# Two transformer blocks on one core: both feed-forwards over all 1024 rows as seven block products, behind all attention

## The chip, the cores and the metric

One core of a Trainium2 chip (trn2). The metric is device time of one execution in microseconds: median 2538.9, three runs from 2533.7 to 2539.64. Engines: TensorE (PE, its weight loads PEld), VectorE (DVE), ScalarE (ACT), GpSimd (POOL), and SyncE (SP), whose queue issues the DMAs.

## The reference

Two different blocks run one after the other on x of 1024 rows x 1024 columns, float32. The first one has 16 more rows in front (`meta`), four heads of differential attention beside a state-space branch; the second has eight heads of causal attention with a forget gate beside a spatial gating branch. Each ends in the same way, and this is what the change touches:

```python
mix = concat(a, b) @ w_out                       # 1024 x 1024
h   = h + rmsnorm(mix, post_mix_g)
n   = rmsnorm(h, pre_ffn_g)
f   = silu(n @ w_gate) * (n @ w_up)              # 1024 x 2816
h   = h + rmsnorm(f @ w_down, post_ffn_g)        # 2816 x 1024
```

## The kernel before

**Matmuls.** Every large product is made of three: each operand is split into hi (rounded to the fp32r type by an ACT copy) and lo (the rest, a DVE subtraction), and hi x hi, hi x lo and lo x hi are summed in one PSUM bank (`mm3`, L106). `wpiece` (L97) brings a weight piece of 128x1024 by DMA into `wr` (2 buffers) and splits it into `wh` and `wl` (4 buffers each); `split` (L169) does the same for what comes out of a transpose.

**Staging.** Attention runs in two halves of 512 rows. In each block the first half (`attention(blk, 0, ...)`) runs beside the projections, and the second half is a generator (`second_half`, L901; `second_half2`, L1190): the last five units of the projections (`dense`), `attention(blk, 1, None)`, then `mix_out` (L769), which brings the attention output (`oD`, `o2D`) and the other branch back from DRAM, transposes them, multiplies by `w_out` and stores rows to `mixD`.

**Feed-forward.** `ffn` (L910) takes two halves of 512 rows. First it drains `mix_out` for rows 0 to 511 and normalises these rows (`norm_row`: `post_norm` L181, `norm_T` L148). Then, for each half, 22 tiles of 128 hidden columns in chunks of 6, 6, 6 and 4: `up` makes gate and up (2 x 8 x 3 matmuls of 128x512), `down` multiplies a chunk by `w_down` for 4 row tiles x 2 column halves and adds into `acc` in SBUF. During half 0 one `step(side)` of the generator above is traced after each tile, so that second-half attention, its mix and the feed-forward of the first half stand side by side. `post_norm` ends each row tile: square and sum on ACT, the power on POOL (L134), a scaling and the residual addition on DVE, a store. Rows 4 to 7 of the second block's input are normalised behind the first block's end (`pre_row`, L1007).

**Attention of a row tile.** `scores` (L607) makes the scores of one map or head in `s` (one PSUM buffer of 128x1024 in this phase), DVE adds the bias and takes the minimum (L626, in the second block after a mask addition L624), ACT takes the exponentials (L632). `transposed_product` (L650) transposes them on PE (L657), copies them to SBUF (L603 on ACT, L605 on DVE, in turn) and multiplies by the values (L118).

**Order.** No order is written by hand. A planner simulates the program at build time and writes each engine's list: what is traced earlier goes first, `ahead()` raises a stretch, and what is not ready in its simulation is passed over. On the chip each engine works its list off in order.

Of the kernel before, what the change touches and what calls it, by code (L numbers as in the profile page):

```python
# [22 lines left out]
KT = 8  # L23
# [7 lines left out]
FF_CHUNKS = [6, 6, 6, 4]  # L31
# [24 lines left out]
def tile_two_blocks(ctx: ExitStack, tc: tile.TileContext, a, out):  # L56
# [4 lines left out]
    wpool = ctx.enter_context(tc.tile_pool(name="wpool", bufs=4))  # L61
# [30 lines left out]
    cD = dram.tile([8, NX], F32, name="cD")  # L92

# [17 lines left out]
    class Bank:  # L111
        """Several sums in one PSUM bank: the first matmul clears it, the last one follows all others."""
# [35 lines left out]
    def norm_T(wk, pt, xt, g_bc, dst, col, np_=128):  # L148
        """Row tile xt [np_, 1024] -> normalised, times g, transposed into dst[hi, lo][:, :, col:col+np_]."""
# [31 lines left out]
    def post_norm(wk, mix, g_bc, res_src, dst, rt, cuts=1):  # L181
        """Row tile mix [128, 1024], normalised, times g, plus the residual; into dst and returned."""
# [3 lines left out]
        hx = wk.tile([128, 1024], F32, tag="hx", name="hx")  # L186
# [16 lines left out]
    # ---------------------------------------------------------------- first block: projections, S5  # L203
# [19 lines left out]
    psum_t = psum(ctx, "t", 2)  # L223
    psum_o = psum(ctx, "o", 1)
    psum_d = psum(ctx, "d", 2)
    psum_e = psum(ctx, "e", 1)
    psum_x = ExitStack()
    psum_s = [psum(psum_x, "s", 2)]

    def psum_phase(width):  # L230
        psum_x.close()
        psum_s[0] = psum(psum_x, "s", 1024 // width, width)

# [11 lines left out]
    rows_out = ctx.enter_context(tc.tile_pool(name="ev", bufs=4, reuse_waits="tile"))  # L245
    atp = ctx.enter_context(tc.tile_pool(name="atp", bufs=2, reuse_waits="tile"))
    lam = ctx.enter_context(tc.tile_pool(name="lam", bufs=1, reuse_waits="tile"))
# [23 lines left out]
    with ExitStack() as pre:  # L271
# [13 lines left out]
        # lambda  # L285
# [13 lines left out]
    # ---- S5 tables  # L299
# [114 lines left out]
    # D on the diagonal of the first tap, [h', g, h]  # L414
# [12 lines left out]
    def ssm_set(s):  # L427
# [15 lines left out]
        # chunk phases E[c], c = 16 a + b  # L443
# [8 lines left out]
        # input map: Gm[p, j, r', h'] = A^(7-r') Bb  # L452
# [8 lines left out]
        # output map: CA[p, j, n, h] = Re(C A^n), -Im(C A^n)  # L461
# [23 lines left out]
        # taps, then the block Toeplitz of a chunk  # L485
# [15 lines left out]
        # u of the set, transposed  # L501
# [19 lines left out]
        # chunk inputs to the states, both parts  # L521
# [53 lines left out]
    def dense1(half):  # L575
# [709 lines left out]
```

## Time and profile before

| | |
|---|---|
| median of 3 runs (lowest, highest) | 2538.9 us (2533.7, 2539.64) |
| span of the profiled execution | 2536.1 us |
| own time of the profiled execution beside its span | not given by the page; the runs' median is 2.8 us above the span |
| PE busy | 2468.3 us, 97% |
| DVE, ACT, POOL busy | 50%, 42%, 12% |
| DMA | 301.59 MB, 119 GB/s |
| mean granted TensorE clock | 0.989 |

A busy matmul counts from its start to a modelled end, and the next one starts before that end; the distance between starts, not the duration, is what one costs. Idle time of an engine that is not the bottleneck costs nothing.

### The profile page before, as it was taken

The numbers are of one execution on the slowest core, as the hardware profiler recorded it, in microseconds if no ns is written. First come the engines' busy times: TensorE is split into PE (matmuls) and PEld (weight loads), VectorE is DVE, ScalarE is ACT, GpSimd is POOL, SyncE is SP. The second block draws the span as 40 slices with busy tenths as digits, with TensorE's granted clock in tenths as the row PEclk, the third lists the DMA queues.
The fourth block names the chain that finished last, engine by engine and source line by source line (L and its number), as shares of the span: only waits on it lengthen the run. The fifth ranks groups of instructions, "written<-read, shape, count | busy, mean of one in ns | idle before, by whom it ended". The sixth has DMA issues, their size and how long they took to land. (4 is left out here: it accounts for less than half of the span.)

```text
span 2536.1 us, 30581 instructions
## 1 busy us (share of the span) xinstructions
PE 2468.3 (97%) x11808; PEld 2015.8 (79%) x11808; DVE 1256.3 (50%) x2035; ACT 1075.9 (42%) x1696; POOL 297.8 (12%) x308
## 2 busy tenths in 40 slices
PE   8998889999999999999999999999999999999998
PEld 6766667888888878888887888888888888888886
DVE  8658764655553374333344546554444426523334
ACT  4334554656452343323224665465543324332222
POOL 1747311110000010000001211010000000000000
PEclk9998999999999999999999999999999999999999
DMA  4432224423223564222246224542322336432322
GB/s 163 143 118 75 86 73 152 142 84 99 77 79 112 187 212 161 90 89 100 93 147 193 70 75 140 189 146 92 111 68 86 106 125 249 160 98 83 108 91 83
DMA packets 122529, 301.59 MB, mean 119 GB/s; under 512 B 25672, under 2 KB 44232, under 8 KB 121872
## 3 DMA queue, kind: packets, MB, share of 16 engines
q1 hardware_dynamic: 122384, 299.64, 36.0%
q8 instruction: 93, 1.52, 0.2%
q14 instruction: 52, 0.43, 0.1%
HBM read 258.44 MB, written 39.98 MB: 118 GB/s over the span
## 5 line engine op out<-in xcount | busy, mean ns | idle before, releaser
L103 DVE TENSOR_TENSOR wl<-wr,wh 128x1024 fp32r<-128x1024 f32 x348 | 431.1, 1240 | 566.6 <-ACT wh L102 553.8
L102 ACT ACTIVATE wh<-wr 128x1024 fp32r<-128x1024 f32 x358 | 379.2, 1060 | 774.9 <-PE e L108 233.2
L107 PE MATMUL d<-wh,fh 128*128 128x512 f32 x704 | 280.3, 399 | 2.5 <-DVE acc L951 2.2
L107 PE MATMUL e<-ffhTh,wh 128*128 128x512 f32 x704 | 277.4, 394 | 1.8 <-ACT ffhTh L171 1.8
L108 PE MATMUL d<-wl,fh 128*128 128x512 f32 x704 | 278.0, 396 | 0.0
L107 PE MATMUL d<-ffhTh,wh 128*128 128x512 f32 x704 | 277.2, 394 | 0.0
L109 PE MATMUL e<-ffhTh,wl 128*128 128x512 f32 x704 | 277.0, 393 | 0.0
L108 PE MATMUL e<-ffhTl,wh 128*128 128x512 f32 x704 | 277.0, 393 | 0.0
L109 PE MATMUL d<-ffhTh,wl 128*128 128x512 f32 x704 | 276.9, 393 | 0.0
L108 PE MATMUL d<-ffhTl,wh 128*128 128x512 f32 x704 | 276.8, 393 | 0.0
L109 PE MATMUL d<-wh,fl 128*128 128x512 f32 x704 | 275.9, 396 | 0.0
L134 POOL TENSOR_TENSOR rs<-rv,mhalf 128x1 f32<-128x1 f32 (+2 forms) x102 | 70.3, 691 | 1668.4 <-DVE rv L133 1659.2
L107 PEld LDWEIGHTS d<-wh,fh 128*128 128x128 f32 x704 | 132.2, 188 | 36.7 <-DVE acc L951 5.9
L107 PEld LDWEIGHTS e<-ffhTh,wh 128*128 128x128 f32 x704 | 132.4, 188 | 30.5 <-ACT ffhTh L171 2.1
L109 PEld LDWEIGHTS d<-wh,fl 128*128 128x128 f32 x704 | 131.9, 188 | 30.9
L108 PEld LDWEIGHTS d<-wl,fh 128*128 128x128 f32 x704 | 132.2, 188 | 30.1
L108 PEld LDWEIGHTS e<-ffhTl,wh 128*128 128x128 f32 x704 | 132.4, 188 | 29.0 <-DVE ffhTl L172 0.5
L109 PEld LDWEIGHTS e<-ffhTh,wl 128*128 128x128 f32 x704 | 132.4, 188 | 28.9
L107 PEld LDWEIGHTS d<-ffhTh,wh 128*128 128x128 f32 x704 | 132.4, 188 | 28.7
L109 PEld LDWEIGHTS d<-ffhTh,wl 128*128 128x128 f32 x704 | 132.4, 188 | 28.7
L108 PEld LDWEIGHTS d<-ffhTl,wh 128*128 128x128 f32 x704 | 132.4, 188 | 28.4
L935 DVE TENSOR_TENSOR sg<-sg,d 128x512 f32<-128x512 f32 x88 | 60.4, 686 | 139.9 <-PE d L109 139.8
(433 smaller groups left out, 4261.3 us busy)
## 6 DMA issues: line engine op xcount, KB each, us to landing
wr<-in_w_gate SPq DMA_DIRECT2D x88, 512.0 KB
wr<-in_w_up SPq DMA_DIRECT2D x88, 512.0 KB
wr<-in_w_down SPq DMA_DIRECT2D x88, 512.0 KB
wr<-in_w_out SPq DMA_DIRECT2D x32, 512.0 KB
hD<-hx SPq DMA_DIRECT2D x24, 512.0 KB
hx<-hD SPq DMA_DIRECT2D x24, 512.0 KB
wr<-in_win_k SPq DMA_DIRECT2D x16, 512.0 KB
wr<-in_win_q SPq DMA_DIRECT2D x16, 512.0 KB
```

The source lines that it names most:

```text
L102: S.activation(out=hi, in_=raw, func=AF.Copy)
L103: (eng or V).tensor_tensor(out=lo, in0=raw, in1=hi.bitcast(F32), op=ALU.subtract)
L107: PE.matmul(out=o, lhsT=l[0], rhs=r[0], start=first, stop=False)
L108: PE.matmul(out=o, lhsT=l[0], rhs=r[1], start=False, stop=False)
L109: PE.matmul(out=o, lhsT=l[1], rhs=r[0], start=False, stop=last)
L134: G.tensor_tensor(out=r[:np_], in0=v[:np_], in1=mhalf[:np_, 0:n], op=ALU.pow)
L935: V.tensor_tensor(out=sg, in0=sg, in1=u, op=ALU.mult)
```

## The change

Rows 0 to 511 and 512 to 1023 become the two halves of one matrix, and each of the three products of a feed-forward is made by Strassen's scheme in Winograd's form: seven products of half-size blocks in place of eight, with sums and differences of blocks as operands.

- `dense` is drained, and the whole second half of attention is traced with the mix of the first rows (`mix_first`), the attention raised by `ahead()`; then `norm_first` puts rows 0 to 511 into `H0`.
- `mix_second` takes rows 512 to 1023 in two pairs of row tiles, keeps the products in SBUF and calls `norm_second`, which forms the five further left operands in `H1`. The eight weight pieces of `w_out` are brought in and split once for each pair.
- `ffn_up` runs 11 hidden tiles of 256 columns x (gate, up): one load of four 128x512 weight blocks, four POOL operations on them, seven splits, seven products of 4 x 3 matmuls into three of eight PSUM banks. Per hidden tile seven left operands of the down product and four of its seven right operands (the other three are the weight blocks themselves) go to DRAM (`fD`, `tD`).
- `ffn_down` is a stage of its own: 7 products x 11 tiles x 4 row tiles x 3 matmuls; each tile loads its left and right operand (256 KB each) and splits both. Sums of products are formed from the banks. `post_norm` of rows 0 to 3 and, in the first block, the normalisation of the next block's first rows stand in products 5 and 6; `post_norm` of rows 4 to 7 follows the last product's row tiles.
- The pools of attention and weights (`open_work`, `close_work`) are closed ahead of `ffn_up` and opened anew after the first feed-forward. Weights are laid out in blocks by the host.

```python
    def mma(o, l, r, first):
        for n, (x, y) in enumerate(((l[0], r[0]), (l[0], r[1]), (l[1], r[0]))):
            PE.matmul(out=o, lhsT=x, rhs=y, start=first and n == 0, stop=True, skip_group_check=True)

    def mix_second(blk, mp, emit):
        ...
        for pr in range(2):
            mTs, xts = [], []
            for i in (4 + 2 * pr, 5 + 2 * pr):
                cat = mp.tile([128, 1024], F32, tag="xn", name="cat")
                ...
                transpose_split(psum_t, cat, mTi, 0, gain=None if blk else subg[:, 0:1])
                ...
            for ch in range(2):
                ws = [wpiece(a["w_out_2" if blk else "w_out"][ch * 4 + i]) for i in range(4)]
                for mTi, xt in zip(mTs, xts):
                    d = psum_d()
                    for k in range(KT):
                        mm3(d, sl(mTi, slice(None), k), kslice(ws, k), k == 0, k == KT - 1)
                    S.activation(out=xt[:, ch * 512:(ch + 1) * 512], in_=d, func=AF.Copy)
            for n, xt in enumerate(xts):
                emit(4 + 2 * pr + n, xt)

    def norm_second(blk, wk, tp, g, rt, H0, H1, xt):
        res, src, _, _ = ffn_args(blk)
        hx = post_norm(wk, xt, g[0], res, src, rt, hb=1)
        ...                                      # normalised and transposed into PSUM t[0], t[1]
        a22 = tmp("a22")
        S.activation(out=a22, in_=t[1], func=AF.Copy)
        split(a22, H1["A22"][0][:, :, c], H1["A22"][1][:, :, c])
        s3 = tmp("s3")
        tsub(V, s3, part(0, 0), t[0])
        tadd(G, s3, s3, part(0, 1))
        s1 = tmp("s1")
        tadd(V, s1, t[0], a22)
        split(s1, H1["S1"][0][:, :, c], H1["S1"][1][:, :, c])
        s2 = a22
        tsub(G, s2, a22, s3)
        ...                                      # split into S2, S3; s4 = part(1, 0) - s2 + part(1, 1), split into S4

    def ffn_up(blk, H0, H1):
        ...                                      # pools: raw 2, units 6, t3 2, sn 5, f 10, wd 1; z: 8 PSUM banks
            def units(raw):
                b11, b12, b22, b21 = (raw[:, i] for i in range(4))
                ...                              # unit(x): a pair of tiles, split(x, hi, lo)
                u["B11"] = unit(b11)
                tsub(G, t3, b22, b12)
                tsub(G, b12, b12, b11)
                tadd(G, b11, b11, t3)
                u["T2"] = unit(b11)
                u["B21"] = unit(b21)
                u["T1"] = unit(b12)
                u["T3"] = unit(t3)
                u["B22"] = unit(b22)
                tsub(G, b21, b21, b11)
                u["T4"] = unit(b21)
                return u
            ...
            for t in range(NT):                  # NT = 11
                ...
                for g in range(2):
                    ...
                    prod(ba, u["B11"], A["A11"], True)
                    S.activation(out=s1, in_=ba, func=AF.Copy)
                    prod(bb, u["T2"], A["S2"], True)
                    tadd(V, u2, bb, s1)
                    prod(ba, u["B21"], A["A12"], False)
                    if g == 0:
                        S.activation(out=f11, in_=ba, func=AF.Silu)
                    else:
                        V.tensor_tensor(out=f11, in0=f11, in1=ba, op=ALU.mult)
                    prod(bc_, u["T1"], A["S1"], True)
                    tadd(V, s15, bc_, s1)
                    prod(bb, u["T3"], A["S3"], False)
                    result(f22, bb, s15)         # a DVE addition, then Silu (g 0) or a DVE product (g 1)
                    prod(bc_, u["B22"], A["S4"], False)
                    result(f12, bc_, u2)
                    prod(bb, u["T4"], A["A22"], False)
                    result(f21, bb, s1)
                ...                              # four POOL operations on f and four on w_down, 11 stores

    def ffn_down(blk, after):
        ...                                      # pools: loads 3 of each kind, operand pairs 6 of each, z: 8 banks
            def operand(src_, e):
                x = rp.tile([128, 512], F32, tag="r" + e, name="r" + e)
                SP.dma_start(out=x, in_=src_)
                p = pair_tile(hp_, [128, 512], "d" + e)
                split(x, p[0], p[1])
                return p
            ...
            groups = [range(0, 4), range(4, 8), range(8, NT)]
            for n, (ai, bn, bank, fresh) in enumerate(...):
                ...
                for gi, grp in enumerate(groups):
                    ops = [(operand(fD[blk][ai, t], "a"), operand(B[bn](t), "b")) for t in grp]
                    for i in range(4):
                        for t, (x, w) in zip(grp, ops):
                            mma(banks[bank][i], sl(x, slice(None), slice(i * 128, (i + 1) * 128)), w,
                                bool(fresh) and t == 0)
                        if gi == 2:
                            evac(n, i)
                    ...

    def feed_forward(blk, side, ffs, fp, mT):
        ...
                for _ in mix_first(blk, mT, rows_):
                    with ahead():
                        step(side, 2)
                H0 = pair_tile(fp, [128, KT, 512], "ffhT", fp_tag[blk])
                for rt in range(4):
                    norm_first(blk, wk, g, rt, H0, rows_[rt])
                    step(side)
            drain(side)
            att_work.close()
            ...
                mix_second(blk, mp, lambda rt, xt: norm_second(blk, mp, tp, g, rt, H0, H1, xt))
            close_work()
            ffn_up(blk, H0, H1)
```

## Rows read from the trace of the kernel before

**Rows 1.** The page's first part: busy time, share of the span, instructions.
```profile
PE 2468.3 (97%) x11808; PEld 2015.8 (79%) x11808; DVE 1256.3 (50%) x2035; ACT 1075.9 (42%) x1696; POOL 297.8 (12%) x308
```
**Rows 2.** Windows: length, busy time of each engine, PE clock, DMA share, GB/s.
```profile
150.00:350.00 200.00, 169.69 (x880) 128.99 (x878) 147.95 (x363) 102.17 (x230) 95.89 (x86) 0.90 0.27 78
376.00:1315.00 939.00, 934.23 (x4294) 765.92 (x4294) 436.31 (x582) 383.77 (x555) 50.33 (x47) 1.00 0.36 120
...
1595.00:2536.00 941.00, 930.34 (x4431) 771.76 (x4429) 412.54 (x543) 365.88 (x496) 40.33 (x42) 1.00 0.36 120
2095.00:2130.00 35.00, 35.00 (x155) 28.71 (x154) 24.22 (x29) 18.36 (x27) 3.29 (x6) 1.00 0.87 322
```
**Rows 3.** The page's costliest groups: busy us, mean ns of one, idle before, releaser.
```profile
L103 DVE TENSOR_TENSOR wl<-wr,wh 128x1024 fp32r<-128x1024 f32 x348 | 431.1, 1240 | 566.6 <-ACT wh L102 553.8
...
L107 PE MATMUL d<-wh,fh 128*128 128x512 f32 x704 | 280.3, 399 | 2.5 <-DVE acc L951 2.2
...
L935 DVE TENSOR_TENSOR sg<-sg,d 128x512 f32<-128x512 f32 x88 | 60.4, 686 | 139.9 <-PE d L109 139.8
```
**Rows 4.** Timeline of PE, up products, first and nineteenth start: start us, us.
```profile
2469.69 0.39 PE L107 MATMUL d<-ffhTh,wh 128*128 128x512 f32 x1
...
2473.81 0.39 PE L107 MATMUL e<-ffhTh,wh 128*128 128x512 f32 x1
```
**Rows 5.** Timeline of PE, down products, first and twenty-fourth start.
```profile
2440.45 0.40 PE L107 MATMUL d<-wh,fh 128*128 128x512 f32 x1
...
2445.82 0.39 PE L109 MATMUL d<-wh,fl 128*128 128x512 f32 x1
```
**Rows 6.** Chain of work that ended last: one head of the second block's attention.
```profile
1912.46 0.81 PE s L619 x4
...
1921.32 0.76 PE t L657 x7
1926.99 1.51 PE o L118 x14
```
**Rows 7.** DVE groups in 1640 to 1961 us, the second block's second-half attention.
```profile
L626 DVE CUSTOM_DVE_ANT_0 s<-s,cb 128x640 f32<-128x640 f32 (+3 forms) x32 | 33.0, 1031 | 0.9
...
L624 DVE TENSOR_TENSOR s<-s,mask 128x128 f32<-128x128 f32 x32 | 9.5, 298 | 39.6 <-PE s L619 39.3
```
**Rows 8.** Timeline of one head's scores, minimum and exponentials.
```profile
1920.34 0.98 PE L619 MATMUL s<-kst,qst 128*128 128x448 f32 x4
...
1921.76 1.10 DVE L626 CUSTOM_DVE_ANT_0 s<-s,cb 128x896 f32<-128x896 f32 x1
...
1922.95 1.01 ACT L632 ACTIVATE P<-s,nm 128x896 f32<-128x896 f32 x1 [0.50 <-DVE nm L626]
```
**Rows 9.** Timeline from the last head's output through DRAM to the mix input.
```profile
1959.54 0.68 DVE L754 TENSOR_TENSOR ob<-o,rl 128x512 f32<-128x512 f32 x1
...
1964.33 0.33 SPq L784 DMA_DIRECT2D cat<-o2D  x1
...
1972.44 0.68 DVE L172 TENSOR_TENSOR mTl<-t,mTh 128x512 fp32r<-128x512 f32 x1
```
**Rows 10.** Timeline of a row tile from its mix product to its normalised rows.
```profile
406.19 0.60 ACT L802 ACTIVATE mrow<-d 128x512 f32<-128x512 f32 x1 [5.30 <-PE d L109]
...
408.87 1.28 DVE L196 SCALAR_TENSOR_TENSOR pn<-mrow,rs,ffg 128x1024 f32<-128x1024 f32 x1 [0.72 <-POOL rs L134]
...
413.50 1.28 DVE L153 SCALAR_TENSOR_TENSOR xn<-hx,rs,ffg 128x1024 f32<-128x1024 f32 x1 [0.72 <-POOL rs L134]
```
**Rows 11.** The same timeline where a POOL operation ran beside DVE.
```profile
415.50 2.41 POOL L103 TENSOR_TENSOR wl<-wr,wh 128x1024 fp32r<-128x1024 f32 x1
415.57 3.42 DVE L196 SCALAR_TENSOR_TENSOR pn<-mrow,rs,ffg 128x1024 f32<-128x1024 f32 x1 [0.72 <-POOL rs L134]
```
**Rows 12.** POOL groups by shape: its 128x512 operation on two tiles.
```profile
L1113 POOL TENSOR_TENSOR vn<-vn,b_ln 128x512 f32<-128x512 f32 x8 | 11.5, 1434 | 8.4 <-DVE vn L1112 8.3
```

More of the change, by code (lines that the diff above doesn't have):

```diff
@@ L92, in tile_two_blocks @@
     cD = dram.tile([8, NX], F32, name="cD")
+    fD = [dram.tile([7, NT, 128, 512], F32, name=f"fD{i}") for i in range(2)]
+    tD = [dram.tile([4, NT, 128, 512], F32, name=f"tD{i}") for i in range(2)]
     def bc(ap, shape):
@@ L767, in attention, with mix_first @@
                 yield
-    def mix_out(blk, half, side, mp=None, mT=None, keep=None):
-        with ExitStack() as ph:
-            mp = mp or pool(ph, "mx", 2, side=side)
-            ready = mT is not None
-            mT = mT or pair_tile(mp, [128, KT, 512], "mT", bufs=1)
-            if blk and not ready:
-                g_b = row_bcast(mp, a["out_norm_b_gain"], 512, "g_b", 1)
-            for i in [] if ready else range(4 * half, 4 * half + 4):
+    def mix_first(blk, mT, keep):
+        yield
+        yield
+        for ch in range(2):
+            ws = [wpiece(a["w_out_2" if blk else "w_out"][ch * 4 + i]) for i in range(4)]
+            for i in range(4):
+                d = psum_d()
+                for k in range(KT):
+                    mm3(d, sl(mT, slice(None), k, slice(i * 128, (i + 1) * 128)), kslice(ws, k),
+                        k == 0, k == KT - 1)
+                S.activation(out=keep[i][:, ch * 512:(ch + 1) * 512], in_=d, func=AF.Copy)
+                yield
+    def mix_second(blk, mp, emit):
+        if blk:
+            g_b = row_bcast(mp, a["out_norm_b_gain"], 512, "g_b", 1)
+        for pr in range(2):
+            mTs, xts = [], []
+            for i in (4 + 2 * pr, 5 + 2 * pr):
                 cat = mp.tile([128, 1024], F32, tag="xn", name="cat")
@@ L899, in tile_two_blocks @@
     psum_phase(1024)
-    def second_half():
-        yield from dense
-        left1.close()
-        yield from attention(0, 1, None)
-        yield from mix_out(0, 1, None)
-    other = second_half()
-    def ffn(blk, side, after, ph, fp, mT):
-        mix, res, src, dst = ((mixD, a["x"], hD[0], hD[1]), (mix2D, hD[1], hD[2], out))[blk]
-        sfx = "_2" if blk else ""
+    def mma(o, l, r, first):
+        for n, (x, y) in enumerate(((l[0], r[0]), (l[0], r[1]), (l[1], r[0]))):
+            PE.matmul(out=o, lhsT=x, rhs=y, start=first and n == 0, stop=True, skip_group_check=True)
@@ L1017, in open, with gain @@
             nT.append(pair_tile(self.p, [128, KT, 512], "nT0"))
-        def run(self, wk, g):
-            gp = wk.tile([128, 1024], F32, tag="ffg1", name="g_pre2a", bufs=1)
-            SP.dma_start(out=gp, in_=a["pre_mix_gain_2"].unsqueeze(0).to_broadcast([128, 1024]))
-            for rt in range(4):
-                pre_row(wk, gp, rt)
-    start2 = Block2Start()
-    ffn(0, other, start2, ffs, fp, mT)
+        def gain(self, wk):
+            self.gp = row_bcast(wk, a["pre_mix_gain_2"], 1024, "g_pre2a", 1)
@@ L1027, in tile_two_blocks, with run @@
+        def run(self, wk, pt, rt):
+            pre_row(wk, self.gp, rt, pt)
+    keep2 = ExitStack()
+    start2 = Block2Start()
+    drain(dense)
+    left1.close()
+    feed_forward(0, attention(0, 1, None), ffs, fp, mT)
+    start2.open()
+    ffn_down(0, start2)
+    open_work(512)
     nTa = start2.p
@@ L1188, in tile_two_blocks @@
     right.close()
-    def second_half2():
-        yield from dense
-        left.close()
-        yield from attention(1, 1, None)
-        yield from mix_out(1, 1, None)
-    ffs = ExitStack()
-    ffn(1, second_half2(), None, ffs, ffn_pool(ffs), mT)
-    psum_x.close()
+    drain(dense)
+    left.close()
+    feed_forward(1, attention(1, 1, None), ExitStack(), nTa, mT)
+    keep2.close()
+    ffn_down(1, None)
 def _cols(w, width=128):
```

307 lines of the change are left out of this document (195 added, 112 removed).

## The prediction

> **What bounds the kernel now.** I read the page's first part, then windows, then the costliest groups, then timelines. PE is busy 97% of the span, no other engine over 50% [rows 1]. From 376 to 1315 us (mix and feed-forward of the first block, with second-half attention) PE is busy 934.2 of 939 us, from 1595 us on 930.3 of 941, and the rest there is mostly the tail; in both stretches DVE and ACT are busy less than half of the time, DMA a third [rows 2]. So these two stretches, three quarters of the span, go at the pace of PE: a matmul taken out is worth its spacing, and every microsecond in which PE has nothing to do is new. The groups say how much is feed-forward: nine groups of 704 matmuls of 128x512 like the one in [rows 3], 6336 together. Their means near 0.4 us are no spacing, since they overlap. The spacing is (2473.81 - 2469.69)/18 = 0.229 us in up products [rows 4] and (2445.82 - 2440.45)/23 = 0.2335 us in down products [rows 5].
>
> **What is removed.** Per block, before: up 2 halves x 22 tiles x 2 x 8 x 3 = 2112 matmuls, down 2 x 22 x 2 x 4 x 3 = 1056. After: up 22 weight blocks x 7 products x 4 x 3 = 1848, down 7 x 11 x 4 x 3 = 924. Saved 264 x 0.229 + 132 x 0.2335 = 91.2 us per block, **182.5 us** in all. The shape (128x512, a new stationary tile each) stays, so I keep the spacing; if all 5544 went at 0.2335, 17 us of it would be gone.
>
> **What is added** is PE idle time: feed-forward matmuls no longer stand beside attention, `mix_out` and the norms. Per block, in order:
>
> *Attention with the first mix.* PE's own work for a head of the second block at 896 keys is 0.81 + 0.76 + 1.51 = 3.08 us [rows 6], and over 640 to 1024 keys 2.86 us on the mean; 32 of them make 92 us, and the 192 matmuls of `mix_first` 44 us: 136 us. Against it stands a chain, for there is one score buffer: scores, minimum and exponentials take 1920.34 to 1923.96, 3.6 us at 896 keys [rows 8], about 3.5 on the mean, 32 x 3.5 = 112 us, and some 12 us for the first load and the last product: 124 us. DVE's largest share in it is 33.0 + 9.5 us [rows 7] and doesn't bound. So in the second block PE still sets the time; I take 6 us of idle. In the first block one transposed product serves two maps: 16 x (2 x 0.81 + 0.76 + 1.51) x 6.5/7 = 58 us and 44 make 102 us by these rows, under the chain of 124; the 16 extra keys add to both. I take 14. Bounds 0 (all hand-offs filled) and 28.
>
> *Into the mix.* The last head's output must go to DRAM, come back and be transposed and split: 1959.54 to 1973.12 us, 13.6 us [rows 9]. Before, PE had feed-forward matmuls there; now only rests of `mix_first` and the transposes of `norm_first`. I take 10 and 11, bounds 0 and 14.
>
> *The mix of the second rows.* 192 matmuls as before, but 16 weight pieces for 8: 8 more x 1.24 us on DVE [rows 3]. While the second pair runs (22 us on PE), DVE has 8 pieces (10 us) and two rows of `norm_second` (3 operations of 1024 columns at 1.28 us [rows 10], seven of 512 at 0.69 [rows 3]: 8.6 us each): 27 us. I take 3 (the rest overlaps pair one), bounds 0 and 10.
>
> *Its tail.* From the copy of the last mix product to the normalised row 406.19 to 414.78, 8.6 us [rows 10]; then transposes (0.9), a DVE subtraction (0.69), two POOL operations (1.43 each [rows 12]) and a split (1.3) until S2, which the second up product needs: 14.4 us, some 17.5 with two rows in the queue. The two products with A11 and A12 need only the first rows: 24 x 0.229 = 5.5 us. I take 12, bounds 0 and 18.
>
> *The up stage.* A weight block has 84 matmuls, 19.2 us. Beside it POOL has eight operations per weight block (its own four, half of the eight on f and `w_down`): 11.5 us at 1.43 [rows 12]; DVE 14 of 512 columns: 9.6 us at 0.69 [rows 3]; ACT about ten copies, 6 us. None is over, but [rows 11] show a DVE operation on two SBUF tiles begun beside a POOL operation: 3.42 us where its like took 1.28 [rows 10], its end following POOL's. Twice per weight block an evacuation has only one product (12 x 0.229 = 2.75 us) until PE needs its bank; behind one split that waits for POOL it takes 1.43 + 0.69 + 0.69 = 2.8. So a loss of a few tenths now and then: 0.7 us per weight block, 15 us. Bounds 0 and 70 (below). At nothing I cost the stores to `fD` and `tD`, which wait for POOL on SP with the next load queued behind: `raw` has two buffers, one weight block (19 us) ahead. Without that cover each hidden tile would lose POOL's four operations, 5.7 us.
>
> *Up to down.* A first load, a split, and four tiles at DVE's 2 x 0.69 = 1.4 us each against PE's 0.7 in the first pass: 7 us; bounds 2 and 14 (the whole round trip of [rows 9]).
>
> *The down stage.* A tile has 12 matmuls, 2.8 us, and needs two splits, 1.4 us on DVE. 154 loads of 256 KB in 216 us are 187 GB/s; [rows 2] show 322 GB/s at a DMA share of 0.87. Operand buffers come free only in the last row tile of a group of four, 0.7 us apart, with two tiles in reserve; I take 1 us per product, 6 us, bounds 0 and 30 (1.4 us at each of 21 groups).
>
> *The end.* Four row tiles leave at 9 x 0.2335 = 2.1 us, and DVE needs an addition of 512 columns and two operations of 1024 for each, 0.69 + 2 x 1.28 = 3.25 us, so it is 5 us behind at the end. Block one: 6 us until the next block's weights are split; block two: 4 us more of tail. Bounds 0 and 13.
>
> *The clock.* From 150 to 350 us PE was busy 85% and its granted clock was 0.90 on the mean of its two levels (1.2 and 2.4 GHz); from 1595 us on, without gaps, 1.00 [rows 2]. Three gaps per block over 7 us will bring it down for a while: 5 us, bounds 0 and 15.
>
> **The sum.** Block one: 14 + 10 + 3 + 12 + 15 + 7 + 6 + 6 + 5 = 78 us. Block two: 6 + 11 + 3 + 12 + 15 + 7 + 6 + 4 + 5 = 69 us. Idle time of before that goes with its stage: 939 - 934 = 5, and 1. Against the profiled span: 2536.1 - 182.5 + 147 - 6 = 2494.6. The page gives the span alone; the median of the runs is 2.8 us above it, and I add that: **2497 us**, 1.6% faster. Of 182 us saved three quarters go to gaps.
>
> **Rivals.**
>
> *A, slower: the up stage goes at DVE's pace.* If each of the 8.5 DVE operations on two SBUF tiles per weight block (7 splits, 1.5 products) waits for a whole POOL operation, DVE needs 9.6 + 8.5 x 1.35 = 21 us for PE's 19.2, and with one exposed evacuation (1.3 us) the weight block takes 22.4: 3.2 us lost instead of 0.7, 44 x 2.5 = 110 us more, 2607. It decides from 0.7 + 42/44 = 1.7 us per weight block. For it: [rows 11], and POOL busy 11.5 of 19.2 us, where in the stretch of the old feed-forward it was busy 50 of 939 us [rows 2]. Against: splits can run several products ahead of PE (six buffers), so a late one need not be felt.
> By the Trainium skill (SBUF — State Buffer, section "SBUF: two separate sides") the port pair that DVE and GpSimd share is an exclusive lock held for a whole instruction, taken by a DVE operation with two SBUF inputs against a GpSimd one that reads SBUF, and the loser fully blocks. By that rule A's time comes out, and the one pair in [rows 11] agrees with it.
>
> *B, slower too: attention and mix don't close up.* If the attention stage pays chain and DVE rests one after the other and the mix waits for both of its rows everywhere, the idle of these four terms goes from 39 and 32 us to the upper bounds, 70 each: 69 us more, 2566. For it: from 150 to 350 us, the stretch in which attention stood beside little else that is dense, PE lost 15% of the time [rows 2]. Against: there DVE was busy 74%, with the state-space work; here it has less.
>
> *C, faster: the gaps are filled.* The planner can pull A11 and A12 products of several weight blocks into the mix tail (eight banks) and `norm_first` and `mix_first` into the round trip; with 4 us left of each of these two (29 us less over both blocks), no loss in up (30) and 3 us per block in down (6), 65 us less: 2432. Against: splits for these products queue on the DVE that the mix tail needs.
>
> *D, it doesn't do what it says:* the matmul spacing rises to 0.2335 or more and the losses come to 180: within 0.3% of before.
>
> **How the numbers follow.** 0.3% is 7.6 us, about what can be told from no change here. Forecast case (2455 to 2530) 0.57, C 0.09, D 0.06, A 0.13, B 0.15. Faster 0.66, within 0.3% 0.06, slower 0.28. The likeliest case's own range is 2455 to 2530. The range for 8 in 10 is 2435 to 2580: it takes in half of C, D and most of B, and leaves out A's upper part. All terms at their lower bounds would give some 2355, which I leave out.
>
> **What will show it.** Right: 5544 matmuls with f, H or d operands at the old spacing; PE busy near 97% in the up and down stages; four gaps of 7 to 15 us per block, at the way into the mix, its tail, between up and down and after down; attention with the first mix lasting 125 to 145 us. A shows as PE waits on DVE in the up stage, with DVE splits of 1.5 to 2.1 us; B as PE busy under 85% from the end of `dense` to the first up product; C as up matmuls that stand before the last mix row is normalised; D as a spacing over 0.2335. The prediction is wrong at its root if the up stage is longer than 22 x 20.5 = 451 us, or the stretch from mix to up over 240 us per block.

## Result, and the profile after

The change makes the kernel slower: 2719.2 us median (2715.7 to 2719.8) against 2538.4, ratio 1.071 [1.070, 1.073]. I had forecast 2497, and faster with a chance of 0.66.

The page of the kernel after, parts 1 and 2:

```profile
span 2717.2 us, 31519 instructions
PE 2361.5 (87%) x11016; PEld 1925.8 (71%) x11016; DVE 1557.9 (57%) x2519; ACT 1097.8 (40%) x1982; POOL 854.0 (31%) x692
...
PE   8988898756499999979979999988548899998997
...
PEclk9999989777699999989989999988669999999999
```

Against [rows 1] PE has 792 instructions fewer and is 106.8 us less busy (2468.3 to 2361.5), but idle 355.7 us instead of 67.8. Where it goes idle, in the eighth to eleventh slice and again in the 29th and 30th, the granted clock falls too.

Windows by stage, both blocks; columns are the stretch, its length, busy us of PE, PE's weight loads, DVE, ACT and POOL, the granted clock, DMA share and GB/s:

```profile
376.00:450.00 74.00, 74.00 (x353) 60.77 (x352) 32.42 (x43) 34.49 (x52) 11.21 (x9) 1.00 0.47 162
450.00:597.00 147.00, 99.42 (x483) 79.43 (x481) 88.10 (x185) 65.66 (x152) 21.13 (x15) 0.79 0.15 49
597.00:615.00 18.00, 5.78 (x25) 4.57 (x25) 11.07 (x16) 6.41 (x11) 1.63 (x3) 0.53 0.62 218
615.00:690.00 75.00, 53.44 (x231) 43.10 (x232) 41.30 (x44) 32.33 (x47) 14.35 (x12) 0.82 0.37 115
690.00:732.50 42.50, 4.35 (x19) 3.19 (x17) 27.66 (x25) 12.83 (x22) 31.86 (x23) 0.54 0.55 198
732.50:900.00 167.50, 151.49 (x624) 122.72 (x625) 99.00 (x105) 47.86 (x81) 117.25 (x81) 0.93 0.54 191
900.00:1178.00 278.00, 277.62 (x1225) 229.55 (x1223) 153.69 (x202) 83.23 (x139) 113.73 (x82) 1.00 0.27 96
1178.00:1193.00 15.00, 0.00 (x0) 0.00 (x0) 1.56 (x3) 1.18 (x3) 5.00 (x4) 0.61 0.89 312
1193.00:1404.00 211.00, 210.97 (x931) 174.66 (x932) 125.13 (x196) 102.17 (x182) 7.02 (x7) 0.99 0.64 215
1404.00:1420.00 16.00, 4.09 (x19) 3.04 (x17) 12.97 (x16) 5.83 (x9) 3.04 (x4) 0.69 0.66 228
...
1778.00:1898.00 120.00, 99.61 (x604) 89.74 (x604) 57.51 (x123) 50.94 (x90) 12.20 (x7) 0.83 0.19 61
1898.00:1918.00 20.00, 6.47 (x30) 5.12 (x31) 14.58 (x22) 9.77 (x20) 3.73 (x6) 0.59 0.46 152
1918.00:1997.00 79.00, 56.64 (x236) 45.27 (x234) 44.17 (x48) 34.58 (x52) 15.47 (x14) 0.78 0.33 107
1997.00:2035.00 38.00, 3.88 (x16) 3.14 (x16) 25.57 (x24) 11.67 (x21) 27.47 (x20) 0.55 0.49 172
2035.00:2180.00 145.00, 126.75 (x517) 101.72 (x518) 74.52 (x86) 39.67 (x67) 100.34 (x70) 0.92 0.56 199
2180.00:2478.00 298.00, 298.00 (x1316) 246.86 (x1315) 170.74 (x219) 91.62 (x154) 133.19 (x94) 1.00 0.30 105
2478.00:2490.00 12.00, 4.97 (x20) 3.83 (x20) 4.45 (x8) 2.19 (x4) 5.01 (x4) 0.80 0.77 235
2490.00:2700.00 210.00, 210.00 (x923) 173.63 (x922) 118.46 (x185) 97.34 (x171) 6.59 (x5) 0.99 0.63 215
2700.00:2717.00 17.00, 0.25 (x2) 0.00 (x0) 10.67 (x15) 2.48 (x6) 2.49 (x3) 0.61 0.51 185
```

Read them in order: the rest of the projections with most of `mix_first` and the first heads of attention; attention alone; into the mix; the mix of the second rows; its tail; the up stage, slow and then full; up to down; down; the end. PE's idle time (length less busy) in block one is 47.6, 12.2, 21.6, 38.2, 16.4, 15.0, 0 and 11.9 us, in block two 20.4, 13.5, 22.4, 34.1, 18.3, 7.0, 0 and 16.8 (its first up product starts at 2039.6 us, so 4.6 of the 18.3 us belong to the tail: 38.7 and 13.7). The steady up and down stages are as full as [rows 2] were.

What PE waited for between attention and the first up products (block one; us in total, times, longest):

```profile
PE t L962 <- DVE xn L956: 29.5, 3, 10.5
PE z L930 <- ACT uh L172: 19.2, 1, 19.2
PE t L962 <- DVE rv L134: 10.3, 1, 10.3
PE t L164 <- DVE rv L134: 7.5, 1, 7.5
PE t L164 <- DVE xn L154: 5.1, 1, 5.1
```

The 39.8 us at L962 are the transposes in `norm_second` (10.3 and 10.5 us for the first pair of row tiles, 8.8 and 10.2 for the second); the 19.2 us are the first split of an up block; the 7.5 and 5.1 us at L164 are norms of the first rows. In attention alone before it (450 to 597 us) PE waited for the exponentials, which free the one score buffer, and for the combination of two maps:

```profile
PE s L634 <- ACT P L647: 33.7, 12, 5.5
PE t L672 <- DVE P L745: 8.6, 7, 5.3
```

### The profile page after: what moved, and what is told of

The parts are those of the page before. It is cut to its first block, busy times and chain, and to the rows that moved or that the text cites. A ratio compares the mean times of both kernels' runs of the same rounds, so it can differ in the third digit from the quotient of the medians.

```text
span 2717.2 us, 31519 instructions
## 1 busy us (share of the span) xinstructions
PE 2361.5 (87%) x11016; PEld 1925.8 (71%) x11016; DVE 1557.9 (57%) x2519; ACT 1097.8 (40%) x1982; POOL 854.0 (31%) x692
## 5 line engine op out<-in xcount | busy, mean ns | idle before, releaser
L172 ACT ACTIVATE uh<-raw 128x512 fp32r<-128x512 f32 x264 | 162.9, 629 | 513.7 <-PE z L930 220.2
L173 DVE TENSOR_TENSOR ul<-raw,uh 128x512 fp32r<-128x512 f32 x264 | 264.1, 1014 | 147.0 <-ACT uh L172 146.9
L930 PE MATMUL z<-dbh,dah 128*128 128x512 f32 x616 | 223.7, 393 | 22.4 <-ACT dbh L172 22.4
L930 PE MATMUL z<-dbh,dal 128*128 128x512 f32 x616 | 236.2, 391 | 0.0
L930 PE MATMUL z<-dbl,dah 128*128 128x512 f32 x616 | 236.1, 391 | 0.0
L104 DVE TENSOR_TENSOR wl<-wr,wh 128x1024 fp32r<-128x1024 f32 x100 | 125.5, 1257 | 131.0 <-ACT wh L103 129.7
L930 PE MATMUL z<-ffhTh,uh 128*128 128x512 f32 x352 | 139.9, 397 | 39.5 <-ACT uh L172 38.5
L103 ACT ACTIVATE wh<-wr 128x1024 fp32r<-128x1024 f32 x110 | 116.4, 1059 | 113.2 <-PE d L109 49.7
L119 PE MATMUL o<-v,at 128*128 128x64 f32 (+1 forms) x864 | 129.5, 301 | 15.7 <-ACT at L618 11.6
L930 PE MATMUL z<-ffhTh,ul 128*128 128x512 f32 x352 | 139.2, 395 | 0.4 <-DVE ul L173 0.4
L930 PE MATMUL z<-ffhTl,uh 128*128 128x512 f32 x352 | 139.1, 395 | 0.0
```

Of the source, the lines that this page charges most:

```text
L103: S.activation(out=hi, in_=raw, func=AF.Copy)
L104: (eng or V).tensor_tensor(out=lo, in0=raw, in1=hi.bitcast(F32), op=ALU.subtract)
L119: i = PE.matmul(out=out, lhsT=lhsT, rhs=rhs, start=not self.seen, stop=last).ins
L172: S.activation(out=h, in_=src, func=AF.Copy)
L173: V.tensor_tensor(out=l, in0=src, in1=h.bitcast(F32), op=ALU.subtract)
L930: PE.matmul(out=o, lhsT=x, rhs=y, start=first and n == 0, stop=True, skip_group_check=True)
```

## The experiments

All ratios are against the kernel before. Theory S: the loss is the staging, since nothing dense stands beside attention and mix any more. Theory O (rival A's kin): the loss is the operand work of the seven products, on POOL, the shared port, SP's queue and through DRAM.

**Staging alone, classical products** (from the kernel before):

```
                 step(side)
+            drain(side)              # all attention and mix_out first
+            if after: after.open()
 ...
-            fb = pool(ph, "fff", 7, side="right")
+            fb = pool(fbs, "fff", 7) # where attention's buffers were
```

> The kernel before, classical products, with only the staging of the change: all second-half attention and its mix are drawn ahead of the feed-forward, in memory that the feed-forward's buffers then take. Theory S (the loss is the staging: attention and mix without feed-forward matmuls beside them): in the kernel after, 450 to 690 us and 1778 to 1997 us held 240 and 219 us for some 125 and 130 us of PE work at full clock; without the 40 us per block that the mix lost to norm transposes, 80 and 50 us of loss stay, so 2538 + 130 = 2670 us (2620 to 2710), with granted clock under 0.85 there. Theory O (the loss is the operand work of the seven products: POOL, shared port, trips through DRAM): at most 2570 us.

2724.9 us, ratio 1.075 [1.072, 1.078]: 15 us above S's range, as slow as the whole change. Its page, part 1, then windows over its attention and mix in both blocks and 200 us of feed-forward:

```profile
span 2720.8 us, 30631 instructions
PE 2523.6 (93%) x11808; PEld 2056.0 (76%) x11808; DVE 1264.8 (46%) x2035; ACT 1008.9 (37%) x1642; POOL 296.3 (11%) x308
```

```profile
450.00:650.00 200.00, 126.90 (x597) 100.12 (x596) 102.20 (x206) 77.78 (x172) 27.35 (x18) 0.77 0.19 61
...
1750.00:1950.00 200.00, 147.97 (x841) 131.38 (x840) 90.11 (x178) 80.63 (x140) 27.13 (x18) 0.80 0.21 67
2100.00:2300.00 200.00, 199.79 (x874) 163.65 (x873) 70.05 (x76) 50.90 (x60) 0.00 (x0) 1.00 0.30 97
```

This run splits the sum. It has the 11808 PE instructions of [rows 1], and they are busy 55.3 us longer (2523.6 - 2468.3): the same work, most of it at a lower clock. An estimate from the traces: busy time times (1 - granted clock), summed over slices of 5 us, comes to 22 us in the kernel before, 69 here and 98 in the kernel after, so the clock covers 47 of the 55. Idle time rises by 129.4 us (197.2 - 67.8); the two stretches shown hold 125 us of it. So staging costs 185 us by itself. Against it the seven products take 162.1 us of PE's busy time away (2523.6 - 2361.5) and bring 158.5 us of new idle time (355.7 - 197.2): both theories hold, each for half, and the change's own gain is gone before it has paid for the staging.

**The second half: mix, tail and start of the up stage.** Three edits of the kernel after: other buffers in the mix; the pools of the up stage in reverse order; the sums of `w_down` left out.

```
-  cat = mp.tile([128, 1024], F32, tag="xn", name="cat")
+  cat = (wpool if pr else mp).tile(..., tag="wr" if pr else "xn", bufs=2)
-  tq = psum_t()...                   # norm_second's transposes
+  tq = psum_s[0]()[:, q * 512:(q + 1) * 512]...
```

> The kernel after, with other buffers in the mix of the second rows: the second pair's input rows come into the weights' landing buffers instead of waiting for the norm's, and the norm's transposes go to the two PSUM banks of the score buffer, so that they don't stand ahead of the second pair's transposes. If the four waits of 10 us per block for xn (PE idle 637.9 to 665 us) are these buffers: PE goes on with pair two, 20 to 27 us less per block, 2719 - 45 = 2674 us (2660 to 2690). If PE waits there for the DVE and POOL chain itself, whatever the order: 2710 to 2725.

2717.2 us, 1.070 [1.067, 1.073]: nothing. PE did more in the mix (67.2 us busy from 597 to 700 us instead of 60.4), but still waited 19.2 us for the first up split, whose load went out at 721.7 us. The wait was real and not the last: what PE gains in the mix it waits for the late load.

> The kernel after, with the order of the up stage's SBUF pools turned round, so that the first raw weight blocks land where the mix's weights were and not where its last rows are; no operation changes. The first up product waited 19.2 us for the split of a block whose load was issued at 724.5 us, behind stores of w_down combinations on SP's queue. If the late load sets the start: the first product comes before 710 us, about 15 us less per block, 2690 us (2680 to 2705). If the chain of norms and S operands sets it (the second product needs S2 of the last row, which came at 722 us): under 5 us per block, 2710 to 2720.

2702.2 us, 1.065 [1.063, 1.067]. The first load went out at 689.8 us instead of 724.5, the first up product ran at 715.8 instead of 732.5 (710 was expected) and the first one with S2 at 724.4 instead of 740.6, 16 us earlier; the whole gained 17 us, not 30. Block one kept its 16 us to the down stage (1177.2 us instead of 1193.0). Block two's first product with S2 came 26.7 us earlier (2021.2 instead of 2047.9), but its down stage only 15.0 (2474.1 instead of 2489.1): the slow part of its up stage took back 12. SP's queue in the kernel after shows what the load had stood behind:

```profile
705.70 0.38 SPq L1087 DMA_DIRECT2D wd<-in_w_down  x1
714.03 0.32 SPq L1094 DMA_DIRECT2D tD<-wx  x1
715.71 6.55 SPq L1094 DMA_DIRECT2D tD<-wd  x3
723.99 0.38 SPq L1087 DMA_DIRECT2D wd<-in_w_down  x1
724.46 0.46 SPq L1043 DMA_DIRECT2D raw<-in_w_gate  x1
```

Three stores of `w_down` sums took 6.55 us to issue, since each waits for POOL, and the weights that PE needs next are behind them.

> The kernel after without the four combinations of w_down per tile (44 POOL operations, 11 loads and 44 stores per block left out; the down stage reads plain blocks of w_down in their place, so the output is not the reference's). Theory O: POOL and its port set the up stage; its two slow starts (151.5 us of PE work in 167.5 us and 126.8 in 145) go, and the mix tail with its POOL chain shortens: 2719 - 2*35 = 2650 us or less. Theory S: only the starts and part of the tail improve, at most 2*15 us: 2690 to 2719, and the up stage after its start stays at 0.23 us per matmul.

2660.5 us, 1.049 [1.046, 1.051]: between the two, 10 us above O's figure and 30 below S's. From 800 to 900 us, the kernel after and this one:

```profile
800.00:900.00 100.00, 89.89 (x373) 73.26 (x374) 61.12 (x67) 28.31 (x50) 69.90 (x48) 0.94 0.51 183
```

```profile
800.00:900.00 100.00, 100.00 (x443) 82.77 (x442) 56.12 (x73) 31.58 (x53) 45.62 (x32) 1.00 0.30 105
```

POOL falls from 69.9 to 45.6 us and PE is full. The DMA share falls too, from 0.51 to 0.30, for the loads and stores of the sums are gone with them; so this run shows what the sums cost, not whether POOL or SP's queue is the part that hurts. Nothing in the up stage needs these sums.

**Work put beside attention.** The two products that need only the first rows (B11 with A11, B21 with A12) drawn beside the second-half attention, results through DRAM:

```
   drain(side)
+  for t in range(NT):                # 24 matmuls per weight block
+      for g in range(2): B11*A11 -> s1 -> sD[t, g]; + B21*A12 -> f11 -> fD[0, t]
-  norm_T(wk, psum_t, hx, g[1], H0, ...)   # norm_first
+  norm_T(wk, psum_e, hx, g[1], H0, ...)
```

> The kernel after, with the two products that need only the first rows (B11 with A11, B21 with A12: 24 matmuls per weight block, 528 per block) taken out of the up stage and drawn beside the second-half attention, their results put into DRAM and fetched in the up stage; the first rows' norm transposes get a PSUM bank of their own so that those rows are ready in time. Theory S (PE stands idle and at half clock because nothing stands beside attention): 2 x 528 x 0.2273 = 240 us of matmuls move into stretches that lost 47 and 20 us idle, some 30 and 25 us of clock and 7 us each on the way into the mix: about 2719 - 135 = 2584 us (2550 to 2620), granted clock over 0.95 in attention. Rival (the attention is bound by DVE and ACT in their queues, and the splits of the filling lengthen it as much as they fill): 2680 us or more.

2648.4 us, 1.042 [1.041, 1.044]: 71 us less, half of what S expected, but well under the rival's 2680. Attention in block one:

```profile
450.00:500.00 50.00, 37.24 (x183) 29.67 (x183) 45.00 (x73) 32.34 (x65) 12.74 (x12) 0.76 0.47 153
500.00:675.00 175.00, 167.11 (x840) 139.66 (x839) 80.33 (x156) 108.17 (x188) 38.66 (x28) 0.98 0.36 119
```

The gaps and the clock are mended (0.79 to 0.98), but attention's last output comes at 679.2 instead of 595.9 us: 528 matmuls, 120 us, cost 83 us there, the first rows' norms with them. By the code the norms needed a bank of their own because `psum_t` turns in the order of the code, which put the first rows' norms behind all of attention; no run has the bank alone.

> The kernel after with only its handovers mended, all products where they were: the mix buffers of the second and the pool order of the third experiment, the combinations of w_down drawn beside attention instead of in the up stage, a PSUM bank of their own for the first rows' norm transposes, and the down stage's landing buffers put where the S operands were released first. If the new idle time that isn't staging (some 159 us: PE idle 356 us after against 197 us in the staged classical kernel) sits in these handovers and in the w_down work: 17 + 59 us as measured one by one, 24 us per block in the mix once the tail doesn't take it back, 7 us per block for the first rows: up to 130 us less, 2610 us (2590 to 2650). If the fixes only push the wait on to the S chain of POOL and DVE: 2660 us or more.

All handovers mended, products where they were: 2667.5 us, 1.051 [1.049, 1.052], 52 us less, not even the 59 us that leaving out the `w_down` sums gave (here they are done, beside attention): the rival's bound (2660 us or more) came true, and the 110 us don't add up. The trace shows where part of it went. With the sums beside it attention lasts 10 us longer in each block (last output at 606.1 instead of 595.9 us; 132.8 instead of 122.2 us from the last product of `mix_first` on in block two), and behind it PE waits 18.2 and 14.1 us for the attention output from DRAM, where the kernel after waited for norms. Both sets together:

> Both of the above in one kernel: first-row products beside attention, and the handovers mended. If staging and handovers are the whole loss and independent: 2719 - 135 - 110 + 15 counted twice = 2490 us (2460 to 2540), under the kernel before (2538), and near the sum that the prediction made. If what one edit wins the other had already (the same DVE and POOL work in fewer gaps): 2560 us or more.

2596.4 us, 1.022 [1.021, 1.024]: 123 us less, as much as 71 + 52, so they add up (the bank for the first rows' norms is in both sets, so its share isn't known), but still slower than before. Attention's end, the mix tail and the up stage:

```profile
675.00:725.00 50.00, 33.35 (x157) 27.10 (x157) 12.80 (x26) 18.16 (x34) 7.29 (x6) 0.86 0.37 127
775.00:800.00 25.00, 3.88 (x16) 3.13 (x16) 20.74 (x20) 9.57 (x16) 14.78 (x12) 0.52 0.31 117
850.00:1075.00 225.00, 225.00 (x995) 186.29 (x994) 156.11 (x190) 66.91 (x109) 149.85 (x100) 1.00 0.48 167
```

The up stage is full although POOL works 150 of 225 us and DVE 156, with five products per weight block instead of seven; in the kernel after, with seven, it is full from 900 us on with POOL at 114 of 278 us. So rival A's steady state did not appear. What is left of PE's idle time in block one sits in attention (39 us from 450 to 700 us) and between its end and the full up stage (45 us from 700 to 850 us).

**The mix tail.** Edits of the last kernel: S sums on DVE (`tadd(V, s3, ...)` for `tadd(G, ...)` and so on); then the first-row products of two or three of the eleven tiles kept for the tail.

> The kernel with both mendings (2596 us), with the four POOL operations per row of the S operands put on DVE, and the norm gains of the mix loaded after its first rows. There, in the mix tail, splits on DVE took 1.75 us beside POOL instead of 0.68, and POOL's own weight combinations stood ahead of the last row's S chain (793 to 809 us), which released the first up product at 812 us. If the shared port and POOL's queue set the tail: 4 x 1.5 us of POOL become 4 x 0.68 of DVE per row and some eight splits get a microsecond shorter, 10 to 15 us per block, 2596 - 25 = 2571 us (2560 to 2580), and the HS splits show 0.7 us. If the chain of norms sets it: within 5 us of 2596.

2582.5 us, 1.017 [1.015, 1.018]: 14 us less, half of what was expected. The splits of S2 and S3 came back to medians of 0.68 us; PE still waits 8.9 and 8.2 us for the last two norms, 9.1 us for the attention output from DRAM and 11.6 us for the first up split.

> The same, with the first-row products of 2 of 11 weight tiles (96 matmuls, 22 us per block) kept for the tail of the mix, ahead of the up stage, in memory that the mix's weights leave. If PE idle in attention and tail is what is left: up to 20 us less per block than f0, 2571 - 35 = 2536 us (2520 to 2560), the same as the kernel before. If their splits on DVE delay the S chain by what they fill: as f0.

2560.8 us, 1.008 [1.007, 1.009], the best of all (six runs from 2554.6 to 2569.0); 22 us less, two thirds of what was expected.

> The same with 3 of 11 tiles (144 matmuls, 33 us per block): 2571 - 45 = 2526 us (2510 to 2555) by the first theory, a little faster than the kernel before; as f0 or slower by the second, since the tail lasts only some 36 us.

2583.8 us, 1.017 [1.016, 1.019]: moving more from attention to the tail loses again; why by 23 us stays open. It isn't attention's length in block one, which ends where it did with two tiles (680.3 and 679.7 us), while the down stage starts 13.7 us later. In the tail of the kernel with two tiles PE still stood 15.5 of 25 us, near half clock (750 to 775 us, busy 9.50, granted clock 0.59), before the norms' transposes. Putting two tiles ahead of these, through the mix's own weight buffers:

> As f2 (2561 us: two of eleven tiles' first-row products kept for the mix tail), but their weights come through the mix's own weight buffers and are drawn ahead of the last rows' norms. In f2 PE stood before the last rows' norm transposes, 8 us twice per block, because the raw blocks that had landed at 750 us were split at 767 us only, behind those norms. If PE's order was the wait: 22 us of matmuls fill the 25 us after the last mix product, 10 to 14 us less per block, 2561 - 24 = 2537 us (2525 to 2550), the same as the kernel before. If DVE and ACT (splits beside the S chain) set the tail: the first up product slips by as much, 2555 to 2570.

2561.8 us, 1.009 [1.007, 1.010]: PE is busy 21.8 of those 25 us, and then waits 16.5 us for the first up split, whose load went out at 771.1 us only. Again a wait in place of a wait.

Six more arrangements of the same work, none better. Three tiles that way:

> The same with three tiles (33 us per block) there and eight beside attention. The tail from the last mix product to the first product with S2 lasted some 30 to 36 us: if PE's order was the wait, as much again as h2 or up to 8 us per block better, 2520 to 2540 us; if attention then lacks its filling (f3 was 23 us slower than f2), 2545 to 2565.

2572.1 us. The next block's norms drawn earlier in the down stage (`range(2)` for `range(2 if n == 6 else 1)`), then one tile that way and one through the up stage's buffers, then one and two:

> As f2 (2561 us), with the first rows' last norms and the next block's first norms drawn two for one from the sixth product of the down stage on, since PE waited 12.0 us for the last of them at the end of block one's down stage: 2551 us (2545 to 2556) if that was PE's order, 2561 if the chain of norms ends there anyway.

> As i1, but of the two tiles kept for the mix tail one comes through the mix's weight buffers ahead of the last norms and one through the up stage's: in f2 PE stood before the last norms, in h2 (both through the mix's buffers) before the up stage's first splits, 16.5 us per block, because those buffers were given back late. If both were order: 10 us per block less than i1, 2531 us (2520 to 2545). If the S chain on DVE sets the tail's end: as i1 within 6 us.

> As i2 with one more tile through the up stage's buffers (eight tiles left beside attention): within 8 us of i2 either way; more than 10 us slower would say that attention needs its filling more than the tail does, as f3 against f2 did.

2571.7, 2564.0 and 2573.2 us: the earlier norms cost 11 us where they should have saved 10 (the wait that they were to shorten, 12.1 us at the end of block one's down stage, grew to 16.6); the order of the tail made 8 us in the second, with intervals that overlap, so little of it is clear of noise. The filling's splits off POOL (`(V, V)` for `(V, G)`), and attention's too:

> As f2 (2561 us), with the second split of each first-row weight block beside attention on DVE (0.69 us) instead of POOL (1.4 us and more). If DVE's waits for the port behind POOL lengthen attention: 5 to 15 us per block less, 2535 to 2550 us. If they cost nothing there, or DVE's own 18 x 0.69 us per block come on top: 2561 to 2575.

> As j1, and the splits of keys and queries of the second-half attention wholly on DVE too, so that POOL there has only the combinations of w_down and the norms' powers. If the port at the change of heads is a part of attention's length: 3 x 1 to 2 us per block less than j1. If DVE is the tighter queue: 5 us or more above j1.

2577.6 and 2576.4 us. The first is 17 us slower, as its second theory has it: the splits cost more on DVE than on POOL. The second is the same as the first and fits neither of its theories.

**Is it PE's half clock that makes attention long?** Six matmuls without a reader behind each head's scores, in the kernel after:

```
+  for _ in range(6 if half else 0):
+      PE.matmul(out=idle, lhsT=qst[:, 0, e, ...], rhs=kst[:, e, 0:512], ...)
```

> The kernel after, with six more matmuls of 128x512 behind each head's scores in the second-half attention (32 x 6 per block, 1.4 us per head at full clock), into a PSUM bank that nobody reads. Attention alone lasted 147 and 120 us, with PE busy 99 us of it at a granted clock of 0.79 and 0.83. If the half clock stretches the chain (scores, transposes, products of each head): the clock there goes to 0.95 or more, the transposes of P come back from 421 to some 275 ns, and the kernel gets 10 to 30 us faster, 2690 to 2710, although PE does 88 us more. If the chain through DVE and ACT sets the pace: the same length within 10 us, 2710 to 2730. If the added matmuls stand in the way in PE's queue: 32 x 1.4 x 2 = 88 us slower at most, 2740 to 2800.

2764.0 us, 1.088 [1.086, 1.090]. The transposes of P in block one's attention, a fixed amount of work, in the kernel after and here (least, median and greatest ns):

```profile
L672 PE MATMUL t<-ident,P x107: 272/421/476, 456.7 to 590.2; 128*128 128x128 f32 x93, 128*16 128x128 f32 x14
```

```profile
L672 PE MATMUL t<-ident,P x103: 270/273/474, 462.0 to 620.0; 128*128 128x128 f32 x90, 128*16 128x128 f32 x13
```

Their median is back at its value at full clock (in block two it was 273 ns in both kernels), and attention's last output still comes 32 us later (628.2 for 595.9), for 45 us of added matmuls. The granted clock of that attention rose only from 0.79 to 0.87 (450 to 629 us), in block two from 0.83 to 0.97 (1808 to 1942 us), and from block one's down stage to the end of block two's attention this kernel takes 22 us longer. So matmuls that only fill PE lose: they stand in its queue, and they wait there themselves (7.4 us for the query splits). How long attention would be at full clock without them isn't shown: 13 of the 45 us went into gaps or were won back by the clock, and this run can't tell which. What the waits above show is the hand-over: 33.7 of the 47.6 us of idle time in block one's attention is PE waiting for ACT to empty the score buffer.

## Why the prediction was wrong, point by point

The steps that failed are the idle terms from attention to the tail, 39 and 32 us in the sum and 120 and 95 us in the trace, and the clock term, 10 us in the sum and 75 in the trace. In both the sum took the uncovered chains for shorter, and for better covered, than they are.

- **Matmuls removed: right.** 5544 at (1004.29 - 999.75)/20 = 0.227 us in the up stage, 182 us as worked out; 162 of it shows as busy time against the staged classical kernel, since more of the rest runs at a lower clock (98 instead of 69 us lost to it, by the estimate above).
- **"Attention with the first mix", 14 and 6 us: failed.** It was 47.6 and 20.4. Two things were wrong in it. The chain of one head was sized too short: 3.5 us taken, but in block one the scores of 27 maps start from 449.2 to 580.0 us, 5.0 us apart, and in block two those of 24 heads from 1779.0 to 1888.2 us, 4.7 apart. The 5.0 contain score products at a lower clock (1.46 instead of 0.76 us for four of 328 columns) and waits of up to 5.5 us at the changes between heads. And the cover was gone by then: 168 of the 192 matmuls of `mix_first` ran before 450 us, beside the rest of the projections and the first five of 32 maps, where PE was full; the first rows' norms ran after attention.
- **"Into the mix", 10 and 11: the size right** (12.2 and 13.5), by luck. PE did not wait for the round trip through DRAM, which I had priced, but 12.6 and 12.3 us for norms of the first rows, which I had counted as cover; the round trip ran beside these, and the transposes of the attention output behind them waited 0.6 us.
- **"The mix of the second rows", 3 and 3: failed**, 21.6 and 22.4. I counted DVE's work and not PE's order: `norm_second`'s transposes, which wait 10 us for a chain of norms, stand in PE's queue ahead of the second pair: 10.3 and 10.5 us of it in block one.
- **"Its tail", 12 and 12: failed**, 38.2 and 38.7. In block one 19.0 us are the norms of the second pair (8.8 and 10.2) and 19.2 us the first up split. I costed one chain of 17.5 us, with 5.5 us of products beside it; but each of the two rows was waited for, and the `w_down` sums, which I put into the up stage, were pulled in, with POOL busy 31.9 of 42.5 us, and held SP's queue ahead of the first load.
- **"The up stage", 15 and 15: the size right** (16.4 and 13.7), the mechanism not: all of it in the first 170 and 145 us, where the sums of `w_down` are made, and none later.
- **"Up to down" 7 and 7, down 6 and 6, the end 6 and 4:** 15.0 and 7.0, 0 and 0, 11.9 and 8 (16.8 us where before it was 8.7 from the last matmul on). Together about right.
- **"The clock", 5 and 5: failed most.** PE's busy time fell by 106.8 instead of 182 us: 75 us. The granted clock accounts for it: 98 us lost in the kernel after against 22 before. I priced three short gaps; it was one stretch per block, 282 and 262 us long, with PE busy 58% and 64% of the time.
- The sum: idle terms 287 us instead of 137; clock 75 instead of 10. -182 + 288 (355.7 - 67.8) + 75 = 181. This adds up by its making, since the 75 is what the busy time lacks; the granted clock is the check on it.

Rival B named the right place and sign (PE busy under 85% from the end of `dense` to the first up product: 163.0 of 282.5 us, 58%), but its bound stopped at 2566: its 70 us of idle time per block were my upper bounds (28, 14, 10 and 18), where 120 and 95 came, and it kept my clock term. The test "wrong at its root if the stretch from mix to up is over 240 us" came true: 282 and 262 us, while the up stage stayed under 451 (445.5 and 438.4).

Rival A's rule was sound, its size not. Its sign did appear: from 732 to 910 us PE waited 13.4 us for DVE (three waits, the longest 6.4) with DVE splits of up to 1.8 us; but the 110 us that it would have cost did not. Beside POOL the splits do take longer: `ul` has a median of 1078 ns, and the same split in the down stage, where POOL is busy 7 of 211 us, 689; in the tail, first beside POOL and then after it:

```profile
719.05 1.74 DVE L173 TENSOR_TENSOR HS3l<-s,HS3h 128x512 fp32r<-128x512 f32 x1
720.94 1.52 DVE L173 TENSOR_TENSOR HS2l<-a,HS2h 128x512 fp32r<-128x512 f32 x1
725.62 0.69 DVE L173 TENSOR_TENSOR HS4l<-s,HS4h 128x512 fp32r<-128x512 f32 x1 [3.15 <-ACT HS4h L172]
```

By the Trainium skill (SBUF — State Buffer, section "SBUF: two separate sides") the engine that starts first holds the shared port pair for its whole instruction, and the other fully blocks. The rows agree, down to one column in attention, which takes 1.22 us beside POOL's 1.80 and ends with it (546.46 and 546.43 us):

```profile
544.63 1.80 POOL L660 TENSOR_TENSOR qst<-qt,qst 64x512 fp32r<-64x512 f32 x1 [12.57 <-ACT qst L658]
545.24 1.22 DVE L645 TENSOR_TENSOR nm<-m 128x1 f32<-128x1 f32 x1
```

In the full part of the up stage, with six operand buffers ahead of PE, it cost PE nothing; whether the buffers are the reason was not tested. In the tail, taking POOL's four operations out of each row (with a later load of the norm gains) was worth 14 us over both blocks.

## What to carry to other kernels

Before dense work is saved or moved, ask what else it was covering: here 182 us of matmuls less were worth nothing, because the same matmuls had hidden two attentions and mixes. Uncovering those cost 185 us in the classical kernel too, and the operand sums and hand-overs of the seven products nearly all of their own gain. Price an uncovered chain with its queues (what stands before it on PE, SP and POOL, and which buffers turn in the order of the code) and with the clock that its gaps bring about, not from its links alone. Keep some independent dense work for each hand-over: this (71 us beside attention, 22 more in the tail) and mended hand-overs (52 and 14 us) won back 158 of the 181 us. Whether an arrangement exists in which the seven products win stays open: none here did.

## What the runs showed of the hardware that was not expected

- The same 11808 PE instructions were busy 55.3 us longer when two stretches of 200 us had gaps (granted clock there 0.77 and 0.80); by the granted clock 47 us of it, a quarter of the staging's 185 us.
- Matmuls added to fill PE brought the transposes' median in block one's attention from 421 to 273 ns, its granted clock from 0.79 to 0.87, and made the kernel 45 us slower: a clock raised in this way did not pay.
- A DVE operation of one column (the median of its 16 at L645 is 0.16 us) took 1.22 us beside a POOL split.
